# Output projection of a hybrid decoder layer: a hand-given order, squares written to SBUF, operand sums on TensorE

## The chip, the cores and the metric

One core of one Trainium2 chip. The metric is the device time of one launch in microseconds (us). Engines are named as in the profile: PE (TensorE, matmul and transpose), PEld (its weight loads), DVE (VectorE), ACT (ScalarE), POOL (GpSimd) and SP (SyncE, which here issues every transfer). Each engine works through its own queue strictly in order, and waits at an instruction whose inputs are not there.

## The reference, cut to what matters

The kernel computes one decoder layer on 1024 tokens of width 1024: a token mixer, a gated feed-forward, and a gated embedding. The change lies between the first two.

```python
mix = concatenate([ret_out, mla_out], -1) @ w_o          # 1024 x 1024
h   = x + rmsnorm(mix, post_mix_norm)
hn  = rmsnorm(h, pre_ffn_norm)
ff  = (silu(hn @ w_gate) * (hn @ w_up)) @ w_down          # inner width 2816
```

## The kernel before

Nearly every product is made three times over, from a high and a low part of each operand (`split`, L79: ACT rounds to the high part, DVE or POOL subtracts to get the low part; `products`, L89: three matmuls for each block of 128 rows).

**The output projection** runs in eight tiles of 128 tokens, in the order 0, 2, 4, 6, 1, 3, 5, 7; tile n below is the n-th of them. Half of the product (`od`) was made earlier and lies in HBM. For each tile `project` (L705) does this in turn:

- ACT and POOL split the attention rows of the tile (`mh`, `ml`), and PE makes 24 matmuls of 512 columns into a pair of PSUM banks (`po3`, two such pairs in turn).
- DVE adds the half from HBM (L715, into `mix`).
- ACT squares `mix` and sums along the row (L717). Its unwanted full-size result goes into the PSUM pair `pt`. DVE and POOL make the reciprocal root (L111, L113).
- DVE scales (L719) and adds `x` (L720, into `ht`); SP stores `ht` as the residual (`hd`).
- ACT squares `ht` (L723, again into `pt`), the root is made, DVE multiplies by the second norm's weights (L725), ACT scales (L726). `mix` now holds the tile of `hn`.

**The gate/up products** use a seven-product scheme on 2 x 2 blocks (Strassen's, Winograd's form), so `hn` is needed as seven operands: B11, B21, T2, T1, T3, B22, T4. Tiles 0 to 3 give the upper block: `operands` (L728) transposes their two halves into B11 and B21 (4 transposes of 128 x 128 each, then an ACT cast and a DVE subtraction, L681 to L688). Tiles 4 to 7 give the other five operands. T1 to T4 are differences, which POOL makes in four subtractions of 128 x 512 (L739 to L742), each before the transposes that read it.

**The gate and up weights** come in pieces of four blocks. `load` brings a piece, `weight_sums` (L791) makes three sums and a difference on POOL, `weight_part` (L798) splits a part on ACT (`gh`) and DVE (`gl`), `product(m, n)` (L820) makes product n of weight matrix m with 12 matmuls, and `evict` takes it out of PSUM. The list `steps` begins with products (0,0), (0,1), (1,0), (1,1), which need B11 and B21 alone. Step (0,2) is the first that needs T2 of all four late tiles and the sums of the weights.

**What sets the order.** A scheduler places the instructions of the output projection and of the first four products, and may mix tiles on each engine as it sees fit. From step 4 on the code stands in `tc.manual_schedule()`, where queues follow the order of the code. SP serves every load and store in one queue. Tile 7's `od` goes into the buffer that tile 4's sums read last (`blk[0]`).

Of the kernel before, what the change touches and what calls it, by code (L numbers as in the profile page):

```python
# [62 lines left out]
def hybrid_layer(ctx: ExitStack, tc: tile.TileContext, a: dict, out: bass.AP):  # L63
    nc = tc.nc
    act, dve, pool, pe, sp = nc.scalar, nc.vector, nc.gpsimd, nc.tensor, nc.sync

    const = ctx.enter_context(tc.tile_pool(name="const", bufs=1))
# [5 lines left out]
    def ps2(name):  # L73
        return ps.tile([P, 2 * 512], F32, tag="s", name=name)
# [117 lines left out]
    xt = load_in(0)  # L192
# [364 lines left out]
    def advance(gen, tag, n):  # L557
        for _ in range(n):
            try:
                gen.send(tag)  # L560
            except StopIteration:
                return
# [118 lines left out]
    def to_operand(i, j, src, tags="tfto"):  # L681
        nonlocal nblk
        pt = ps1("ptx", tags[nblk % len(tags)])
        nblk += 1
        for k in range(4):
            pe.transpose(pt[:, k * P : (k + 1) * P], src[:, k * P : (k + 1) * P], ident)
        js = slice(j * P, (j + 1) * P)
        split(xs[i][0][:, :, js], xs[i][1][:, :, js], pt.rearrange("p (k n) -> p k n", k=4))  # L688

# [7 lines left out]
    def load_rows(n):  # L697
        sp.dma_start(out=mts[n], in_=mo[order[n]])

    def load_tiles(n):  # L700
        t = order[n]
        sp.dma_start(out=blk[n % 7], in_=od[t])
        sp.dma_start(out=blk[7 + n % 3], in_=a["x"][t * P : (t + 1) * P])

    def project(n):  # L705
        t = order[n]
        mt = mts[n]
        mh, ml = [pmo.tile([P, 4, P], F32R, name=n_) for n_ in ("mh", "ml")]
        mix, ht = blk[n % 7], blk[7 + n % 3]
        split(mh, ml, mt, sub=pool)  # L710
        pt = ps2("po3")
        for c in range(2):
            cs = slice(c * 512, (c + 1) * 512)
            products(pt[:, cs], [(mh[:, k, :], ml[:, k, :], wo2[k][0][:, cs], wo2[k][1][:, cs]) for k in range(4)])
        dve.tensor_tensor(out=mix, in0=pt, in1=mix, op=ALU.add)  # L715
        ss = small.tile([P, 1], F32, name="s3")
        act.activation(pt, mix, AF.Square, accum_out=ss)  # L717
        rsqrt(ss, ss, 1.0 / D)
        dve.scalar_tensor_tensor(out=mix, in0=mix, scalar=ss, in1=wpm, op0=ALU.mult, op1=ALU.mult)  # L719
        dve.tensor_tensor(out=ht, in0=ht, in1=mix, op=ALU.add)  # L720
        sp.dma_start(out=hd[t], in_=ht)
        ss = small.tile([P, 1], F32, name="s3")
        act.activation(pt, ht, AF.Square, accum_out=ss)  # L723
        rsqrt(ss, ss, 1.0 / D)
        dve.tensor_tensor(out=mix, in0=ht, in1=wpf, op=ALU.mult)  # L725
        act.activation(mix, mix, AF.Copy, scale=ss)  # L726

    def operands(n, part=None):  # L728
        j = n % 4
        mix = blk[n % 7]  # L730
        if n < 4:
            to_operand(B11, j, mix[:, lo_])
            to_operand(B21, j, mix[:, hi_])
        else:
            e, ht = blk[j], blk[7 + n % 3]
            t1, t2, t3, t4 = e[:, lo_], ht[:, lo_], mix[:, lo_], e[:, hi_]
            b11, b12, b21, b22 = e[:, lo_], mix[:, lo_], e[:, hi_], mix[:, hi_]
            if part != 1:
                pool.tensor_tensor(out=t1, in0=b12, in1=b11, op=ALU.subtract)  # L739
                pool.tensor_tensor(out=t2, in0=b22, in1=t1, op=ALU.subtract)  # L740
                pool.tensor_tensor(out=t3, in0=b22, in1=b12, op=ALU.subtract)
                pool.tensor_tensor(out=t4, in0=b21, in1=t2, op=ALU.subtract)  # L742
            for i, src in ((T2, t2), (T1, t1), (T3, t3), (B22, b22), (T4, t4))[slice(*((0, 5), (2, 5), (0, 2))[part or 0])]:
                to_operand(i, j, src)

    load_rows(0)
    load_rows(1)
    load_tiles(0)
    for v, name in ((wpm, "w_post"), (wpf, "w_pref")):
        sp.dma_start(out=v, in_=a[name].broadcast_to([P, D]))  # L750
    for n in range(1, 4):
        if n > 1:
            load_rows(n)
        if n < 3:
            load_tiles(n)
    for n in range(NT):
        if n == 7:
            load_tiles(7)
        project(n)
        if n % 4 < 2:  # L760
            load_rows(n + (4 if n < 4 else 2))
        if n >= 2:
            operands(n - 2)
        if n < 4:
            load_tiles(n + 3)
    st_m.close()
    st_b.close()

# [29 lines left out]
    def weight_part(m, p):  # L798
        nonlocal nparts
        r, s = graw[m % 2], gs[m % 2]  # L800
        src = (r[:, 0:2], s[:, 0:2], r[:, 2:4], s[:, 2:3])[p]
        hi, lo = [v[:, : src.shape[1]] for v in ghl[nparts % 4]]
        nparts += 1
        split(hi, lo, src)
        parts[m, p] = hi, lo
# [84 lines left out]
    load(1)  # L890
    weight_part(0, 0)
    weight_part(1, 0)
    operands(NT - 2)
    for m, n in steps[:2]:
        product(m, n)
    operands(NT - 1, 2)
    for m, n in steps[2:4]:
        product(m, n)
    for m in range(2):
        weight_sums(m)  # L900
    for m, n in steps[:4]:
        evict(m, n)
# [45 lines left out]
    with tc.manual_schedule():  # L948
        for i, (m, n) in enumerate(steps):
            if i < 4:  # L950
                continue
            for f, args in todo[i]:
                f(*args)
            if i == 6:
                operands(NT - 1, 1)
            product(m, n)
            evict(m, n)
    st_g.close()
# [209 lines left out]
```

## Time and profile before

| | |
|---|---|
| median of 3 runs | 1400.54 us (1399.19 to 1403.55) |
| the profiled execution | 1400.68 us, span 1398.9 us |
| mean granted PE clock over the span | 0.986 |
| busy share of the span | PE 96%, PEld 81%, DVE 55%, ACT 39%, POOL 33% |
| output projection's first and last matmul start | 571.91 and about 635 us |
| first gate/up matmul, and step (0,2) | 644.73 and 671.25 us |
| PE without a gap again from | 671.25 us |

The profile is one execution seen from the chip. A row of a timeline has the start (us from the start of the span), the length, engine, line, operation, what is written and read, how many such instructions in a row; in brackets how long the engine had been idle before it, and what ended that. PE rows overlap, because matmuls are pipelined. A 128 x 128 float32 matmul stands as two records, a transpose as one.

### The profile page before, as it was taken

The page shows a single profiled execution, that of the slowest core. Times are in us where ns is not written, and L with a number is a line of the kernel's source. Part 1 is how long each engine was busy: PE and PEld are TensorE (multiplying, and loading weights), DVE is VectorE, ACT ScalarE, POOL GpSimd, SP SyncE. Part 2 cuts the span into 40 slices and gives each one's busy share as a digit, 9 for nine tenths or more (in the row PEclk, how much of TensorE's full clock was granted, in tenths as well). Part 3 has the DMA queues.
Part 4 walks back from the last instruction along what each step waited for, and adds up shares of the span by engine and source line. Part 5 has one row for each costly group of instructions (what it writes and reads, how often), then busy time and mean ns, then how long its engine had stood idle before and what let it go on. Part 6 is the DMA issues. An engine that isn't in the chain of part 4 may idle for free.

```text
span 1398.9 us, 18091 instructions
## 1 busy us (share of the span) xinstructions
PE 1336.5 (96%) x6756; PEld 1134.4 (81%) x6756; DVE 770.9 (55%) x1193; ACT 541.8 (39%) x898; POOL 461.8 (33%) x341
## 2 busy tenths in 40 slices
PE   7999999999989999887999999999999999999997
PEld 6987988988778887665788888888888788888886
DVE  6445637445566676488445444444445554474645
ACT  5443321011565555355343333333334444344521
POOL 1100000000363333248577666666664100012500
PEclk9999999999999999998999999999999999999999
DMA  7127831212474641743344344433346876565422
GB/s 251 46 92 250 265 118 39 75 23 60 143 232 123 200 131 30 273 135 123 121 165 149 146 173 173 169 138 144 140 178 218 269 234 211 178 218 193 138 102 75
DMA packets 85304, 214.73 MB, mean 153 GB/s; under 512 B 8992, under 2 KB 23840, under 8 KB 79584
## 3 DMA queue, kind: packets, MB, share of 16 engines
q1 hardware_dynamic: 85216, 213.58, 45.5%
q8 instruction: 53, 0.87, 0.3%
q14 instruction: 35, 0.29, 0.1%
HBM read 144.86 MB, written 67.63 MB: 152 GB/s over the span
## 4 chain that ended last, share of the span: by engine, by line
PE 83%; DMA 4%; DVE 4%; POOL 3%; issue 3%; ACT 2%; SPq 1%; DVEq 0%; ACTq 0%; POOLq 0%
PE gu L834 29%; PE db L1011 7%; PE pqk L94 6%; PE pg L94 6%; PE da L1011 6%; PE pa L94 4%; PE fill L94 3%; PE prv L94 3%; PE sc L94 3%; PE ptp L630 2%; PE prg L94 2%; PE pge L94 2%; PE po L642 1%; PE pq L94 1%; PE po L641 1%
## 5 line engine op out<-in xcount | busy, mean ns | idle before, releaser
L834 PE MATMUL gu<-x,gh 128*128 128x512 f32 x1232 | 383.6, 393 | 6.3 <-ACT po L723 5.6
L834 PEld LDWEIGHTS gu<-x,gh 128*128 128x128 f32 x1232 | 233.2, 190 | 55.7 <-ACT po L723 5.8
L834 PE MATMUL gu<-x,gl 128*128 128x512 f32 x616 | 241.2, 392 | 0.4 <-DVE gl L82 0.4
L834 PEld LDWEIGHTS gu<-x,gl 128*128 128x128 f32 x616 | 116.7, 189 | 25.1 <-DVE gl L82 0.7
L845 ACT COPY duo<-gu 128x512 f32<-128x512 f32 x66 | 38.9, 589 | 189.3 <-PE gu L834 189.3
L621 POOL TENSOR_TENSOR pr<-pr,ri 128x128 f32<-128x128 f32 (+3 forms) x64 | 74.8, 1178 | 105.7 <-DVE ri L620 98.4
L113 POOL TENSOR_TENSOR s<-s,mhalf 128x1 f32<-128x1 f32 x32 | 23.9, 752 | 238.4 <-DVE s L111 238.3
L113 POOL TENSOR_TENSOR gf<-gf,mhalf 128x4 f32<-128x4 f32 x8 | 8.1, 1008 | 266.7 <-DVE gf L111 266.7
L82 DVE TENSOR_TENSOR gl<-strip,gh 128x1024 fp32r<-128x1024 f32 (+1 forms) x44 | 61.6, 1399 | 33.3 <-ACT gh L81 33.3
L82 DVE TENSOR_TENSOR x<-draw,x 128x1024 fp32r<-128x1024 f32 (+1 forms) x43 | 48.1, 1135 | 46.9 <-ACT x L81 46.9
L82 DVE TENSOR_TENSOR gl<-graw,gh 128x1024 fp32r<-128x1024 f32 x22 | 33.8, 1538 | 72.5 <-ACT gh L81 72.5
L81 ACT CAST x<-draw 128x1024 fp32r<-128x1024 f32 (+1 forms) x47 | 45.2, 979 | 73.0 <-PE db L1011 20.6
L82 DVE TENSOR_TENSOR gl<-duo,gh 128x1024 fp32r<-128x1024 f32 x22 | 29.5, 1343 | 67.9 <-ACT gh L81 67.9
L850 DVE TENSOR_TENSOR duo<-gu,duo 128x512 f32<-128x512 f32 x66 | 45.4, 687 | 38.0 <-PE gu L834 37.9
L82 DVE TENSOR_TENSOR tl<-ptp,th 128x512 fp32r<-128x512 f32 (+1 forms) x80 | 49.8, 633 | 24.7 <-ACT th L81 23.7
L94 PE MATMUL pg<-x,x 128*128 128x512 f32 (+1 forms) x255 | 58.9, 378 | 0.0
L81 ACT CAST th<-ptp 128x512 fp32r<-128x512 f32 (+1 forms) x80 | 42.4, 544 | 41.9 <-PE ptp L630 41.6
L855 POOL TENSOR_TENSOR duo<-duo 128x512 f32<-128x512 f32 x11 | 23.3, 2122 | 103.2 <-DVE duo L818 103.2
L617 ACT ACTIVATE pr<-sc,nm 128x128 f32<-128x128 f32 (+3 forms) x64 | 47.7, 747 | 18.7 <-DVE nm L612 11.1
L94 PEld LDWEIGHTS pg<-x,x 128*128 128x128 f32 x255 | 45.8, 188 | 8.6
L612 DVE CUSTOM_DVE_ANT_0 sc<-sc,cmask 128x128 f32<-128x128 f32 (+3 forms) x64 | 48.0, 770 | 7.7 <-PE sc L94 7.3
L94 PE MATMUL pqk<-bl,hi_r 128*128 128x512 f32 x128 | 50.7, 396 | 0.0
(368 smaller groups left out, 3418.5 us busy)
## 6 DMA issues: line engine op xcount, KB each, us to landing
draw<-ld SPq DMA_DIRECT2D x58, 256.0 KB, 3.8
graw<-in_w_gate SPq DMA_DIRECT2D x11, 1024.0 KB, 8.6
duo<-in_w_up SPq DMA_DIRECT2D x11, 1024.0 KB, 4.7
duo<-in_w_down SPq DMA_DIRECT2D x11, 1024.0 KB, 5.1
td<-duo SPq DMA_DIRECT2D x11, 1024.0 KB, 4.4
ld<-duo SPq DMA_DIRECT2D x11, 1024.0 KB, 4.4
draw<-td SPq DMA_DIRECT2D x36, 256.0 KB, 4.1
ld<-duo SPq DMA_DIRECT2D x11, 768.0 KB, 6.7
```

Source lines behind the costliest of these rows:

```text
L81: act.copy(out=hi, in_=src)
L82: sub.tensor_tensor(out=lo, in0=src, in1=hi.bitcast(F32), op=ALU.subtract)
L94: pe.matmul(dst, l, r, start=(m == 0), stop=(m == n - 1))
L113: pool.tensor_tensor(out=dst, in0=dst, in1=mhalf[:, :n], op=ALU.pow)
L612: dve.tensor_tensor_reduce(out=sv, in0=sv, in1=cmask[:, S - n :].rearrange("p (c n) -> p c n", c=nc_), scale=-1.0, scalar=3.0e38, op0=ALU. ...
L617: act.activation(pr_[:, :n].rearrange("p (c n) -> p c n", c=nc_), sv, AF.Exp, bias=nm, scale=-1.0, accum_out=rs)
L621: pool.tensor_tensor(out=pr_[:, :n], in0=pr_[:, :n], in1=ri.broadcast_to([P, n]), op=ALU.mult)
L630: pe.transpose(pt[:, m * P : (m + 1) * P], pb[qq][:, kk * P : (kk + 1) * P], ident)
L834: pe.matmul(dst, l[:, at, ks], r[:, k, :], start=(n in (0, 1, 3) and x == 0), stop=(x == 11), skip_group_check=True)
L845: act.copy(out=s[nm], in_=dst)
L850: dve.tensor_tensor(out=s[nm], in0=dst, in1=s[nm], op=ALU.add)
L1011: pe.matmul(banks[j], l[:, ls], r[:, rs_], start=(fresh and q == 0 and m == 0), stop=(q == NQ - 1 and m == 2), skip_group_check=True)
```

## The change

It does five things.

1. `project` and `operands` are cut into `prepare`, `out_product`, `squares`, `sums`, `operand_list` and `turn`, and all of it, up to the first four gate/up products, stands in `tc.manual_schedule()`. In `turn(n)` three tiles are at work: tile n's norms, tile n-1's last scaling and sums, and tile n-2's operands. The matmuls of tile n+1 are queued behind tile n-2's transposes.
2. Both squares write their unwanted result to SBUF (`junk`, 8 x 128 columns in the T4 operand) and no longer to the PSUM pair.
3. POOL makes two sums a tile and not four (T1 and T3). T2 and T4 are summed by PE: a float32 matmul with the identity, or with its negative `minus`, for each of their 2 or 3 terms, added up in PSUM. For tiles 4 to 7 this makes 8 and 12 matmuls (16 and 24 records) of what were 4 and 4 transposes.
4. `minus` is made once by DVE near the program's start.
5. `load(1)`, tile 7's `od` and the weight parts stand at given places.

```diff
-        act.activation(pt, mix, AF.Square, accum_out=ss)
...
+            for n, v in enumerate(src):
+                pe.matmul(pt[:, ks], v[:, ks], (ident, minus)[n % 2], start=(n == 0), stop=(n == len(src) - 1))
...
+    def squares(n, i, v):
+        ss = roots[n, i] = small.tile([P, 1], F32, name="s3")
+        act.activation(junk, v.rearrange("p (b n) -> p b n", b=8), AF.Square, accum_out=ss)
+
+    def sums(n):
+        e, mix, ht = blk[n % 4], blk[n % 7], blk[7 + n % 3]
+        pool.tensor_tensor(out=ht[:, lo_], in0=mix[:, lo_], in1=e[:, lo_], op=ALU.subtract)
+        pool.tensor_tensor(out=ht[:, hi_], in0=mix[:, hi_], in1=mix[:, lo_], op=ALU.subtract)
...
+        return [(T2, j, (b22, t1)), (T1, j, (t1,)), (T3, j, (t3,)), (B22, j, (b22,)), (T4, j, (b21, b22, t1))]
...
+    def turn(n):
+        mix, ht = blk[n % 7], blk[7 + n % 3]
+        own, last = n < NT, 1 <= n
+        ops = operand_list(n - 2) if n >= 2 else []
+        if own:
+            dve.tensor_tensor(out=mix, in0=banks_o[n], in1=mix, op=ALU.add)
+        if last:
+            rsqrt(roots[n - 1, 1], roots[n - 1, 1], 1.0 / D)
+        for o in ops[:2]:
+            to_operand(*o)
+        if own:
+            squares(n, 0, mix)
+        if last:
+            act.activation(blk[(n - 1) % 7], blk[(n - 1) % 7], AF.Copy, scale=roots[n - 1, 1])
+        if own:
+            rsqrt(roots[n, 0], roots[n, 0], 1.0 / D)
+        if n - 1 >= 4:
+            sums(n - 1)
+        for o in ops[2:]:
+            to_operand(*o)
+        if own:
+            if n + 2 < NT:
+                prepare(n + 2)
+            if n + 1 < NT:
+                out_product(n + 1)
+            dve.scalar_tensor_tensor(out=mix, in0=mix, scalar=roots[n, 0], in1=wpm, op0=ALU.mult, op1=ALU.mult)
+            dve.tensor_tensor(out=ht, in0=ht, in1=mix, op=ALU.add)
+            sp.dma_start(out=hd[order[n]], in_=ht)
+            squares(n, 1, ht)
+            dve.tensor_tensor(out=mix, in0=ht, in1=wpf, op=ALU.mult)
...
+        for n in range(NT - 1):
+            turn(n)
+            if n < 4:
+                load_tiles(n + 3)
+            if n in (2, 3):
+                load_rows(n + 4)
+            if n == 6:
+                load_tiles(7)
...
+    with tc.manual_schedule():
+        turn(NT - 1)
+        load(1)
+        weight_part(0, 0)
+        for m, n in steps[:2]:
+            product(m, n)
+        turn(NT)
+        weight_part(1, 0)
+        for m, n in steps[2:4]:
+            product(m, n)
+        for o in operand_list(NT - 1)[:2]:
+            to_operand(*o)
+        for m in range(2):
+            weight_sums(m)
```

Three places show what moves. SP's queue at the last tiles, before (`hd` is a store of the residual, `duo<-od` and `duo<-in_x` are loads of a tile, `graw<-in_w_gate` is the first gate weights' load):

```order
L703 DMA duo_5742<-in_x 128x1024
L721 DMA hd_91<-duo_5742 128x1024
L789 DMA graw<-in_w_gate 128x2048
L702 DMA duo_5741<-od_109 128x1024
L789 DMA duo_5738<-in_w_up 128x2048
L721 DMA hd_93<-duo_5742 128x1024
```

and in the change:

```order
L773 DMA hd_88<-duo_5744 128x1024
L773 DMA hd_90<-duo_5741 128x1024
L773 DMA hd_92<-duo_5744 128x1024
L710 DMA duo_5743<-od_110 128x1024
L711 DMA duo_5744<-in_x 128x1024
L823 DMA graw<-in_w_gate 128x2048
L773 DMA hd_94<-duo_5744 128x1024
L823 DMA duo_5740<-in_w_up 128x2048
```

Tile 7's `od` stands behind tile 6's store in both. Its `x` moved behind that store, the gate weights behind both loads, and the up weights behind tile 7's store.

ACT's queue from the last tile's norms to the first parts of the weights, before (`x_5730` to `x_5734` are T2, T1, T3, B22, T4; `gh` casts are parts of the weights; L717 and L723 are tile 7's squares):

```order
L81 CAST gh_6262<-graw 128x1024
L81 CAST x_5733<-ptx 128x4x128
L81 CAST x_5731<-ptx 128x4x128
L717 ACTIVATE po_6173,s_6199<-duo_5741 128x1024
L81 CAST x_5730<-ptx 128x4x128
L81 CAST gh_6256<-duo_5738 128x1024
L81 CAST x_5732<-ptx 128x4x128
L845 COPY duo_5739<-gu 128x512
L723 ACTIVATE po_6173,s_6206<-duo_5742 128x1024
```

and in the change (`x_5732` to `x_5736` are now T2, T1, T3, B22, T4; L729 is tile 7's second square, L759 its last scaling):

```order
L729 ACTIVATE x_5736,s_6289<-duo_5744 128x8x128
L81 CAST gh_6223<-graw 128x1024
L81 CAST x_5732<-ptx 128x4x128
L81 CAST x_5733<-ptx 128x4x128
L759 ACTIVATE duo_5743<-duo_5743,s_6289 128x1024
L81 CAST x_5734<-ptx 128x4x128
L81 CAST x_5735<-ptx 128x4x128
L81 CAST x_5736<-ptx 128x4x128
L81 CAST gh_6217<-duo_5740 128x1024
L81 CAST gh_6219<-strip 128x1024
L81 CAST gh_6221<-strip 128x1024
L81 CAST x_5732<-ptx 128x4x128
```

The cast of the first gate part moved from before tile 7's squares to behind both of them. Tile 7's own T2 cast (the last row) stands behind the casts of the summed parts `gh_6219` and `gh_6221` of both weight matrices.

POOL's queue at the same place, before (L739 to L742 are tile 7's sums, L793 to L796 the sums of weights, L113 the roots):

```order
L793 TENSOR_TENSOR strip<-graw 128x512
L794 TENSOR_TENSOR strip<-strip,graw 128x512
L796 TENSOR_TENSOR graw<-graw 128x512
L795 TENSOR_TENSOR strip<-graw,strip 128x512
L794 TENSOR_TENSOR strip<-strip,duo_5738 128x512
L113 TENSOR_TENSOR s_6206<-s_6206,mhalf 128x1
L795 TENSOR_TENSOR strip<-duo_5738,strip 128x512
L739 TENSOR_TENSOR duo_5741<-duo_5741 128x512
```

and in the change (L733 and L734 are tile 7's sums, L827 to L830 the sums of weights):

```order
L113 TENSOR_TENSOR s_6289<-s_6289,mhalf 128x1
L733 TENSOR_TENSOR duo_5744<-duo_5743 128x512
L734 TENSOR_TENSOR duo_5744<-duo_5743 128x512
L827 TENSOR_TENSOR strip<-graw 128x512
L828 TENSOR_TENSOR strip<-strip,graw 128x512
L829 TENSOR_TENSOR strip<-graw,strip 128x512
L830 TENSOR_TENSOR graw<-graw 128x512
L827 TENSOR_TENSOR strip<-duo_5740 128x512
L828 TENSOR_TENSOR strip<-strip,duo_5740 128x512
```

The sums of weights moved from before tile 7's last root and sums to behind them.

## Rows read from the trace of the kernel before

**Rows 1.** Who waited for whom, 575 to 700 us: total us, times, longest.
```profile
PE po L94 <- ACT po L723: 9.2, 6, 3.6
...
PE gu L834 <- ACT po L723: 5.6, 1, 5.6
```

**Rows 2.** Stretches: us, busy time by engine, then granted PE clock, DMA share, GB/s.
```profile
600.00:610.00 10.00, 7.56 (x22) 6.00 (x23) 7.24 (x9) 3.82 (x6) 1.16 (x3) 0.66 0.55 182
...
670.00:680.00 10.00, 9.32 (x33) 6.93 (x32) 2.30 (x2) 2.53 (x4) 4.97 (x5) 0.68 0.30 105
680.00:690.00 10.00, 10.00 (x49) 8.40 (x48) 6.41 (x8) 4.97 (x10) 8.21 (x6) 1.00 0.86 285
```

**Rows 3.** Chain that ended last, from step 4 of the gate/up products on.
```profile
680.87 59.20 PE gu L834 x261
```

**Rows 4.** Timeline of DVE in the output projection.
```profile
578.06 1.22 DVE L715 TENSOR_TENSOR duo<-po,duo 128x1024 f32<-128x1024 f32 x1 [5.26 <-PE po L94]
...
597.65 1.28 DVE L719 SCALAR_TENSOR_TENSOR duo<-duo,s,strip 128x1024 f32<-128x1024 f32 x1 [0.66 <-POOL s L113]
598.97 2.17 DVE L720 TENSOR_TENSOR duo<-duo,duo 128x1024 f32<-128x1024 f32 x1
601.06 1.21 DVE L715 TENSOR_TENSOR duo<-po,duo 128x1024 f32<-128x1024 f32 x1
...
606.71 1.23 DVE L720 TENSOR_TENSOR duo<-duo,duo 128x1024 f32<-128x1024 f32 x1
...
613.70 1.27 DVE L82 TENSOR_TENSOR x<-ptx,x 128x512 fp32r<-128x512 f32 x2
...
627.52 1.21 DVE L715 TENSOR_TENSOR duo<-po,duo 128x1024 f32<-128x1024 f32 x1
...
646.33 1.21 DVE L715 TENSOR_TENSOR duo<-po,duo 128x1024 f32<-128x1024 f32 x1
```

**Rows 5.** Timeline of ACT: a square and its sum, a scaling, a cast of weights.
```profile
595.64 1.05 ACT L717 ACTIVATE po<-duo 128x1024 f32<-128x1024 f32 x1
596.60 0.20 ACT L717 ACTIVATION_READ_ACCUMULATOR po<-duo 128x1 f32 x1
...
614.44 1.15 ACT L726 ACTIVATE duo<-duo,s 128x1024 f32<-128x1024 f32 x1 [0.15 <-POOL s L113]
...
677.31 1.05 ACT L81 CAST gh<-graw 128x1024 fp32r<-128x1024 f32 x1
```

**Rows 6.** Timeline of POOL: a low part of the rows, and a sum of weights.
```profile
598.58 1.48 POOL L82 TENSOR_TENSOR ml<-strip,mh 128x512 fp32r<-128x512 f32 x1 [0.96 <-ACT mh L81]
...
660.26 1.28 POOL L795 TENSOR_TENSOR strip<-graw,strip 128x512 f32<-128x512 f32 x1
```

**Rows 7.** Timeline of PE: float32 matmuls (two records each), projection, transposes, gate/up.
```profile
333.21 1.05 PE L475 MATMUL pu<-vt,kz 128*128 128x128 f32 x8
...
585.16 0.50 PE L94 MATMUL po<-bh,mh 128*128 128x512 f32 x1 [2.21 <-ACT po L723]
...
602.44 0.79 PE L94 MATMUL po<-bh,mh 128*128 128x512 f32 x1 [3.58 <-ACT po L723]
603.03 0.63 PE L94 MATMUL po<-bl,mh 128*128 128x512 f32 x1
...
644.73 0.71 PE L834 MATMUL gu<-x,gh 128*128 128x512 f32 x2
...
671.25 1.52 PE L834 MATMUL gu<-x,gh 128*128 128x512 f32 x2 [0.68 <-ACT x L81]
...
679.39 1.47 PE L686 MATMUL ptx<-pack,duo 128*128 128x128 f32 x12
680.62 0.71 PE L834 MATMUL gu<-x,gh 128*128 128x512 f32 x2
```

**Rows 8.** DMA issues with KB and us to landing: tile 7's `od`, and an `x` alone.
```profile
duo<-od SPq DMA_DIRECT2D x1, 512.0 KB, 7.3
...
duo<-in_x SPq DMA_DIRECT2D x1, 512.0 KB, 3.6
```

More of the change, by code (lines that the diff above doesn't have):

```diff
@@ L123, in hybrid_layer @@
     mhalf = const.tile([P, 32], F32, name="mhalf")
+    minus = const.tile([P, P], F32, name="minus")
     pool.memset(mhalf, -0.5)
@@ L654, in hybrid_layer @@
     act.activation(small.tile([P, 1], F32, name="warm", bufs=1), rs, AF.Silu)
+    dve.tensor_scalar(out=minus, in0=ident, scalar1=-1.0, scalar2=None, op0=ALU.mult)
     advance(gen, "f", 2 * NT)
@@ L685, in to_operand @@
         for k in range(4):
-            pe.transpose(pt[:, k * P : (k + 1) * P], src[:, k * P : (k + 1) * P], ident)
+            ks = slice(k * P, (k + 1) * P)
+            if len(src) == 1:
+                pe.transpose(pt[:, ks], src[0][:, ks], ident)
+                continue
+            for n, v in enumerate(src):
+                pe.matmul(pt[:, ks], v[:, ks], (ident, minus)[n % 2], start=(n == 0), stop=(n == len(src) - 1))
         js = slice(j * P, (j + 1) * P)
@@ L703, in load_tiles, with prepare, out_product @@
         sp.dma_start(out=blk[7 + n % 3], in_=a["x"][t * P : (t + 1) * P])
[L705 to L711, printed above, removed]
+    junk = xt[6][:, :, :, 3 * P :].rearrange("p h k n -> p (h k) n")
+    split_rows, banks_o, roots = {}, {}, {}
+    def prepare(n):
+        split_rows[n] = [pmo.tile([P, 4, P], F32R, name=n_) for n_ in ("mh", "ml")]
+        split(*split_rows[n], mts[n], sub=pool)
+    def out_product(n):
+        mh, ml = split_rows[n]
+        pt = banks_o[n] = ps2("po3")
         for c in range(2):
@@ L714, in project, with operand_list @@
             products(pt[:, cs], [(mh[:, k, :], ml[:, k, :], wo2[k][0][:, cs], wo2[k][1][:, cs]) for k in range(4)])
-        dve.tensor_tensor(out=mix, in0=pt, in1=mix, op=ALU.add)
-        ss = small.tile([P, 1], F32, name="s3")
-        act.activation(pt, mix, AF.Square, accum_out=ss)
[L718 to L728, printed above, removed]
+    def squares(n, i, v):
[5 more added lines that the diff above has]
+        pool.tensor_tensor(out=ht[:, hi_], in0=mix[:, hi_], in1=mix[:, lo_], op=ALU.subtract)
+    def operand_list(n):
         j = n % 4
@@ L731, in operands @@
         if n < 4:
[L732 to L744, printed above, removed]
+            return [(B11, j, [mix[:, lo_]]), (B21, j, [mix[:, hi_]])]
+        e, ht = blk[j], blk[7 + n % 3]
+        b21, b22, t1, t3 = e[:, hi_], mix[:, hi_], ht[:, lo_], ht[:, hi_]
+        return [(T2, j, (b22, t1)), (T1, j, (t1,)), (T3, j, (t3,)), (B22, j, (b22,)), (T4, j, (b21, b22, t1))]
[29 more added lines that the diff above has]
+            dve.tensor_tensor(out=mix, in0=ht, in1=wpf, op=ALU.mult)
     load_rows(0)
@@ L750, in hybrid_layer @@
         sp.dma_start(out=v, in_=a[name].broadcast_to([P, D]))
[L751 to L765, printed above, removed]
+    load_rows(2)
+    load_tiles(1)
+    load_rows(3)
+    load_tiles(2)
+    with tc.manual_schedule():
+        prepare(0)
+        load_rows(4)
+        prepare(1)
+        load_rows(5)
+        out_product(0)
+        for n in range(NT - 1):
[6 more added lines that the diff above has]
+                load_tiles(7)
     st_m.close()
@@ L889, in hybrid_layer @@
     load(0)
[L890 to L902, printed above, removed]
+    with tc.manual_schedule():
+        turn(NT - 1)
[11 more added lines that the diff above has]
+            weight_sums(m)
+        for m, n in steps[:4]:
+            evict(m, n)
     for q in range(NQ):
@@ L951, in hybrid_layer @@
                 continue
+            if i == 6:
+                for o in operand_list(NT - 1)[2:]:
+                    to_operand(*o)
             for f, args in todo[i]:
                 f(*args)
-            if i == 6:
-                operands(NT - 1, 1)
             product(m, n)
```

## The prediction

> **What bounds the kernel now.** I read the chain that ended last first. From step 4 of the gate/up products on it is PE alone: 261 matmuls in 59.20 us, 0.227 each, without a gap [rows 3]. The stretches say the same: PE is busy 10.00 of 10 us in 680 to 690, but 7.56 of 10 in 600 to 610 [rows 2]. So whatever brings step (0,2) forward or back moves the rest of the kernel by as much, and only the stretch from 572 to 680 us counts. Next I read who waits for whom there: PE waits 9.2 us for ACT's second square (L723) to release the projection's PSUM pair, and 5.6 us more for the same line before the first products of the up weights [rows 1]. These waits are what the change can take. The timelines of the engines then give the price of every piece. In the projection, DVE starts a new tile (L715) at 578.06 for tile 0 and at 627.52 for tile 6, 8.2 us a tile, and tile 7 follows only at 646.33 [rows 4]. Yet PE has only 24 matmuls and 8 transposes to do for an early tile: 24 x 0.227 + 8 x 0.10 = 6.2 us (12 transposes take 1.23 from 679.39 to the product's start at 680.62 [rows 7]).
>
> **The change, part by part.** I follow the new queues to the start of step (0,2).
>
> *Tiles 0 to 6.* With the squares in SBUF, PE no longer waits for ACT. But what is late next is the norm's own chain, which no order shortens. From L715's start: the square begins after 1.24, takes 1.21 with its sum [rows 5], and 0.85 later (596.80 to 597.65) L719 starts [rows 4, 5]. L719 to L720 is 1.32, L720 takes 2.09 (598.97 to 601.06), L725 some 1.14. This is 7.85 us. Beside the first two steps DVE's two operand subtractions, 1.27 [rows 4], fit. I take 2.09 for L720 because in the new order POOL's low part `ml` for tile n+2 waits for ACT's cast behind the last scaling, and so falls on L719 and L720 in each turn, as the `ml` of 598.58 fell on the L720 of 598.97. Undisturbed, L720 took 1.23 at 606.71 [rows 4, 6]. The square's new form, float32 to strided SBUF, is in no row. Its nearest rows are the square to PSUM, 1.05, and the scaling to SBUF, 1.15 [rows 5]: I add 0.1. Six turns of 7.95 are 47.7, and turn 5 pays 1.3 more for POOL's first sums beside DVE: tile 6's L715 starts at 578.1 + 47.7 + 1.3 = 627.1, against 627.52. **Nothing is gained here.**
>
> *Tile 7's load.* SP's queue holds tile 7's `od` behind tile 6's store, and that behind tile 6's L720. In the new DVE queue L719 and L720 of tile 6 stand behind all five operands of tile 4. PE's part of these is 16 + 4 + 4 + 4 + 24 = 52 records. Eight float32 records took 1.05 [rows 7], about 0.11 each with the last one's tail left out: 5.8 us. They begin when T1's sum is there, at about 623.7, and end at 629.5, or at 631.9 if the clock has fallen by then. With cast and subtraction, L719 runs at about 633, L720 ends at 635.6, and the load is issued at 636. Alone 512 KB landed in 3.6, beside a load of weights in 7.3 [rows 8]. Here a store and `x` run with it, which is nearer to the first: I take 5. Tile 7's L715 starts at 641.2, **5.1 earlier** than 646.33 [rows 4].
>
> *The first gate product.* Here the order loses. Before, it started at 644.73 [rows 7], ahead of tile 7's L715. Now its weight cast stands on ACT behind both of tile 7's squares, and these behind tile 5's operands: after L715 one subtraction gives T4 its PSUM bank (1.8), T4's 24 records take 2.7, its cast and subtraction 1.4, L719 1.5, L720 1.2, the square 1.2, the cast 1.05 [rows 4, 5, 7]. That is 11 us: start at **652.2**, 7.5 later.
>
> *To the last scaling.* Two products are 24 matmuls, 5.4. PE has then been idle for some 6 us. In the rows, after an idle of 3.58 us the matmuls of 602.44 and 603.03 stand at 0.79 and 0.63, where that of 585.16, after 2.21, stands at 0.50, and the granted clock of 600 to 610 is 0.66: 2.4 GHz for a part of it and 1.2 for the rest [rows 2, 7]. At 1.2 GHz a matmul takes 0.227 more. I add 2.4, about eleven such matmuls. T2 of tile 6, 16 records, follows at 660.0 and ends at 661.8. Its cast and T1's are 1.1, and then ACT comes to tile 7's scaling, 1.15 [rows 5], at **664.1**.
>
> *POOL's tail.* Behind that scaling POOL has two sums for tile 7 and then the weight sums of both matrices, of which six must be done before the second matrix's part can be cast. Eight times 1.33 (one takes 1.28 [rows 6]) is 10.7. Two meet a DVE subtraction of weights, 1.1 each, as `ml` and L720 met [rows 4, 6]. This ends at 677.0. The cast takes 1.05 [rows 5], and T2 of tile 7 stands behind it on ACT, and behind that part's subtraction on DVE: 0.5 + 1.1 + 0.7 more. Step (0,2) starts at **680.4**, 9.1 after 671.25 [rows 7].
>
> *Behind it.* T3, B22 and T4 of tile 7 are now 32 records, 3.6 us, where 12 transposes took 1.23 [rows 7]: 2.4 more on PE. The low clock after 671.25 (0.68 in 670 to 680 [rows 2]) was paid before and is paid again, since PE idles ahead of (0,2) as it did.
>
> The sum: 9.1 + 2.4 = **11.5 us**, against the profiled execution's 1400.68: 1412.2, and the median shown is 0.14 lower. I say **1412**.
>
> *At nothing:* `minus`, one 128-wide DVE instruction while the program's first loads are awaited, under 0.3 us were it bare. POOL's eight sums fewer: POOL waits for the scaling, not for itself, until the tail. The extra records of tiles 4 and 5 lie under the wait for tile 7's `od`. If that cover went, they would cost 40 x 0.11 = 4.4 us, of which 4 are in the sum already, through L719 of tile 6.
>
> *Bounds.* Float32 matmuls that ran one by one, at about 0.2 a record, would add some 4 us on the path. At half my price they'd take off 2.5. The square's form: 0 to 1. The load of `od`: 3.6 to 7.3, so -1.4 to +2.3. The clock: two falls of 2.4, neither or both. The meetings of POOL and DVE: from none (-9, below) to one more in each late turn (+4).
>
> **Rivals.** *Faster: POOL and DVE do not meet, and the clock stays up.* Then L720 is 1.23 in seven turns (-6), the sums and the weight sums meet nothing (-3.5), the first products run at 2.4 GHz, before (0,2) too (-4.8), and the load comes early (-1.4): 1412 - 15.7 = **1396**. For it: before, L720 met `ml` only in some turns, and 606.71 shows the clean one. Against it: in the new order `ml` is released just there in every turn. It decides for this case if five or more of the eight L720 are under 1.3. The Trainium skill (SBUF — State Buffer, section "SBUF: two separate sides") says that DVE and GpSimd lock their shared SBUF ports for a whole instruction, so whoever starts first blocks the other. By this an `ml` that came after L720's start would only hand the same delay to L725, and the turn would stay as long; the trace agrees, with 2.17 against 1.23.
>
> *About even: half the meetings vanish and one fall of the clock,* 1412 - 8 = **1404**.
>
> *Slower still: PE's clock falls in the projection itself.* PE idles about 1.7 us in each turn of 7.95. If that were enough to hold the clock down, 24 matmuls at 0.45 are 10.9 us with 8 transposes 1 to 2 more, and PE would set a turn of 12: six turns give 6 x 4 = 24, of which the wait for tile 7's load hides 4: **1432**. For it: the row of 602.44. Against: after the 2.21 of 585.16, more than a turn's single gaps, the matmul stood at 0.50 [rows 7].
>
> *The change doesn't do what it says:* the queues show that it does, but for the weight casts ahead of tile 7's T2, which is in the sum.
>
> **How the numbers follow.** A measurement of this kernel tells about 0.3% (4.2 us) from no change. The forecast, 1406 to 1420, has 0.70, all of it slower. The even case has 0.13, half within 0.3% and half slower. The fast rival has 0.11, of which 0.09 is faster and 0.02 the same. The slow one has 0.06. Sums: faster 0.09, same 0.09, slower 0.82. The range that leaves out the fast rival and most of the slow one is 1400 to 1423.
>
> **What would show it.** Right: L715 of tile 6 near 627 and of tile 7 near 641; L720 near 2.1 in most turns; the first gate product at 652, PE idle for 5 us and more ahead of it; tile 7's scaling at 664; POOL at work without a gap from there for 12 us; step (0,2) near 680. Wrong: a turn of 7 us or less, or step (0,2) before 672, which would make the change even or faster. PE's wait for ACT's square should be gone in any case.

## The result, and the profile after

| | before | the change |
|---|---|---|
| median of the runs of the first comparison | 1400.27 us (5 runs) | 1413.74 us (5 runs, 1406.31 to 1416.29) |
| ratio, with 95% interval | | 1.0091, 1.0067 to 1.0115 |
| the profiled execution, its span | 1400.68, 1398.9 | 1406.31, 1404.5 |
| PE busy, granted PE clock over the span | 96%, 0.986 | 96%, 0.991 |
| DVE, ACT, POOL busy | 55%, 39%, 33% | 55%, 39%, 32% |

The change is slower by 0.7 to 1.2%. Its profiled execution happens to be the quickest of the five; a second series with a second profile stands below (`change_again`: 1.0069, 1.0046 to 1.0093). As tile 0's first add (L715, now L751) starts at another time in each execution, the text counts from there. Three stretches then make the span: up to that add (578.06 before, 574.92 in the change), from it to ACT's copy of product (0,3) (108.33 and 116.78), and the rest (712.5 and 712.8). **The change shows in the middle one.** The first wanders by more than its 3.1 between executions (last section).

Who waited for whom from 572 to 690 us in the change (us in total, times, longest), where [rows 1] had PE waiting for ACT's squares:

```profile
POOL duo L733 <- ACT duo L759: 10.5, 4, 9.8
...
PE gu L868 <- ACT gh L81: 7.6, 2, 6.0
...
DVE duo L751 <- DMA duo<-od: 3.6, 1, 3.6
...
PE gu L868 <- DVE duo L884: 2.4, 1, 2.4
```

PE's waits for the squares are gone. In their place PE waits 6.0 for the first gate part's cast, POOL 9.8 for tile 7's scaling, and DVE 3.6 for tile 7's `od`. The chain of waits of the change joins these (start, length, engine, what is written, line; pieces under 0.4 us are left out, other cuts are marked):

```profile
631.53 1.23 DVE duo L772
633.21 4.34 DMA duo<-od
637.63 1.22 DVE duo L751
...
645.09 1.24 DVE duo L772
646.41 1.15 ACT x L729 x2
647.56 0.94 ACT gh L81
648.52 1.22 DVE gl L82
649.82 6.48 PE gu L868 x22
656.30 1.80 PE ptx L694 x16
658.12 1.07 ACT x L81 x2
659.20 1.05 ACT duo L759
660.32 1.27 POOL duo L733
...
671.31 1.29 POOL strip L828
672.62 1.05 ACT gh L81
673.70 1.33 DVE gl L82
675.03 1.20 DVE x L82 x2
676.23 0.61 DVE duo L884
676.88 5.75 PE gu L868 x24
682.63 0.87 PE ptx L690 x8
683.50 2.68 PE ptx L694 x24
686.18 73.94 PE gu L868 x326
```

It is one serial chain through five engines: tile 6's residual, tile 7's load, its norms, the gate cast, both first products, tile 6's T2, tile 7's scaling, eight POOL operations in a row, a cast, two subtractions, an eviction (L884), and only then step (0,2) at 676.88. From 686.18 on PE is alone, as in [rows 3].

DVE, ACT, PE and POOL of the change, timelines that answer to [rows 4, 5, 7, 6]:

```profile
590.92 1.22 DVE L751 TENSOR_TENSOR duo<-po,duo 128x1024 f32<-128x1024 f32 x1
...
594.30 1.28 DVE L771 SCALAR_TENSOR_TENSOR duo<-duo,s,strip 128x1024 f32<-128x1024 f32 x1 [0.73 <-POOL s L113]
595.62 2.18 DVE L772 TENSOR_TENSOR duo<-duo,duo 128x1024 f32<-128x1024 f32 x1
...
598.98 1.22 DVE L751 TENSOR_TENSOR duo<-po,duo 128x1024 f32<-128x1024 f32 x1
```

```profile
646.41 1.06 ACT L729 ACTIVATE x<-duo 128x1024 fp32r<-128x1024 f32 x1 [3.27 <-DVE duo L772]
...
674.07 1.07 ACT L81 CAST x<-ptx 128x512 fp32r<-128x512 f32 x2 [0.39 <-PE ptx L694]
```

```profile
648.54 1.22 PE L868 MATMUL gu<-x,gh 128*128 128x512 f32 x2 [6.03 <-ACT gh L81]
...
676.88 0.73 PE L868 MATMUL gu<-x,gh 128*128 128x512 f32 x2 [2.42 <-DVE duo L884]
```

```profile
595.07 1.65 POOL L82 TENSOR_TENSOR ml<-strip,mh 128x512 fp32r<-128x512 f32 x1 [0.80 <-ACT mh L81]
...
664.12 2.28 POOL L828 TENSOR_TENSOR strip<-strip,graw 128x512 f32<-128x512 f32 x1
```

The square to SBUF takes 1.06, to PSUM it took 1.05 [rows 5]. L772 of 595.62 met POOL's low part of 595.07 and took 2.18, and a turn is 8.06 (590.92 to 598.98). Two stretches (busy us of PE, PEld, DVE, ACT and POOL, then the granted clock) answer to [rows 2]: 640 to 650 is the gap before the first product, and in 670 to 680, where before had 0.68, the clock is now 1.00.

```profile
640.00:650.00 10.00, 3.94 (x26) 3.02 (x25) 7.18 (x10) 4.77 (x9) 3.09 (x4) 0.78 0.37 133
...
670.00:680.00 10.00, 7.58 (x44) 6.41 (x43) 4.51 (x6) 3.78 (x7) 6.00 (x4) 1.00 0.00 0
```

### The profile page after: what moved, and what is told of

The parts are those of the page before. It is cut to its first block, busy times and chain, and to the rows that moved or that the text cites. A ratio compares the mean times of both kernels' runs of the same rounds, so it can differ in the third digit from the quotient of the medians.

```text
span 1404.5 us, 18353 instructions
## 1 busy us (share of the span) xinstructions
PE 1344.7 (96%) x6884; PEld 1143.5 (81%) x6884; DVE 770.0 (55%) x1194; ACT 541.1 (39%) x898; POOL 445.4 (32%) x333
## 4 chain that ended last, share of the span: by engine, by line
PE 83%; DVE 5%; issue 4%; ACT 3%; POOL 2%; DMA 2%; SPq 1%; DVEq 0%; ACTq 0%; POOLq 0%
PE gu L868 29%; PE db L1049 8%; PE pqk L94 6%; PE pg L94 6%; PE da L1049 6%; PE pa L94 4%; PE fill L94 3%; PE prv L94 3%; PE sc L94 3%; PE ptp L631 2%; PE prg L94 2%; PE pge L94 2%; PE pq L94 1%; PE po L643 1%; DVE duo L772 1%
## 5 line engine op out<-in xcount | busy, mean ns | idle before, releaser
L113 POOL TENSOR_TENSOR s<-s,mhalf 128x1 f32<-128x1 f32 x32 | 23.9, 750 | 265.8 <-DVE s L111 265.8
L113 POOL TENSOR_TENSOR gf<-gf,mhalf 128x4 f32<-128x4 f32 x8 | 8.1, 1006 | 266.7 <-DVE gf L111 266.7
L884 DVE TENSOR_TENSOR duo<-gu,duo 128x512 f32<-128x512 f32 x66 | 45.4, 688 | 38.8 <-PE gu L868 37.5
```

Source lines behind the costliest of these rows:

```text
L884: dve.tensor_tensor(out=s[nm], in0=dst, in1=s[nm], op=ALU.add)
```

## The experiments

Theory: the order around tile 7 and the first products costs the time. Rivals: the extra float32 records on PE, the squares' new place, and POOL's tail or PE's clock alone. "Kernel before" means the runs of it on the same chip in the same series. The kernel before had a median of 1400.27 in the first series, 1398.14 beside `change_again` to `weight_sums_first`, 1396.07 beside `low_part_dve` to `sums_alone`, 1398.25 beside `scheduled` and `two_norms`, and 1395.76 beside the last two: compare ratios, not medians, across series. The last four columns are starts in us after tile 0's first add, from one profile each ("scaling" is tile 7's last):

| kernel | median | ratio to before (95%) | tile 7's add | scaling | step (0,2) | copy of (0,3) |
|---|---|---|---|---|---|---|
| before | 1400.27 | 1 | 68.27 | 86.70 | 93.19 | 108.33 |
| the change | 1413.74 | 1.0091 (1.0067 to 1.0115) | 62.71 | 84.17 | 101.96 | 116.78 |
| change_again | 1408.85 | 1.0069 (1.0046 to 1.0093) | 62.78 | 87.09 | 104.87 | 121.32 |
| gate_first | 1407.15 | 1.0059 (1.0039 to 1.0078) | 63.32 | 80.72 | 98.50 | 114.91 |
| pool_sums | 1408.33 | 1.0060 (1.0037 to 1.0083) | 66.84 | 88.18 | 103.10 | 117.31 |
| weight_sums_first | 1410.08 | 1.0077 (1.0058 to 1.0095) | 62.80 | 84.21 | 101.71 | 116.52 |
| low_part_dve | 1408.28 | 1.0094 (1.0066 to 1.0121) | 62.03 | 84.63 | 102.41 | 118.83 |
| load_first | 1407.18 | 1.0092 (1.0064 to 1.0119) | 59.56 | 83.46 | 101.25 | 117.70 |
| squares_alone | 1397.91 | 1.0018 (1.0000 to 1.0037) | 65.02 | 86.06 | 92.65 | 107.94 |
| sums_alone | 1396.01 | 1.0008 (0.9989 to 1.0027) | 62.96 | 77.29 | 87.52 | 103.33 |
| scheduled | 1396.37 | 0.9986 (0.9970 to 1.0003) | 63.15 | 83.02 | 90.56 | 105.96 |
| two_norms | 1390.58 | 0.9937 (0.9913 to 0.9962) | 56.39 | 69.16 | 87.88 | 100.93 |
| tail_only | 1401.72 | 1.0040 (1.0024 to 1.0056) | 64.29 | 76.01 | 95.10 | 111.49 |
| head_only | 1407.20 | 1.0076 (1.0056 to 1.0096) | 56.43 | 80.06 | 97.84 | 114.27 |

The first seven below "before" are the change, or the change with one edit. `squares_alone`, `sums_alone` and `scheduled` are the kernel before with parts of the change. The last three have a mended hand order.

**change_again**: the change, unedited.

> The change once more, for its spread. From tile 0's first add (L751) to the start of step (0,2) the change took 101.96 us in its profile, the kernel before 93.19. If the order costs the time, this stretch is again 102 within 1 us and the median again near 1413. If the loss is only in where PE's clock falls, the stretch changes by more than 3 us between two profiles of the same kernel.

Neither came true as written. The order's stretch is long again, but 104.87 is not within 1 us of 102, nor is the median near 1413; and the two profiles of one kernel differ by 2.9 in it, not by more than 3, though by 4.5 up to the copy of (0,3). PE in this profile:

```profile
640.77 0.78 PE L694 MATMUL ptx<-pack,duo 128*128 128x128 f32 x2 [2.13 <-DVE x L82]
...
651.37 1.22 PE L868 MATMUL gu<-x,gh 128*128 128x512 f32 x2 [6.03 <-ACT gh L81]
...
680.92 0.73 PE L868 MATMUL gu<-x,gh 128*128 128x512 f32 x2 [4.03 <-DVE duo L884]
...
682.94 1.05 PE L868 MATMUL gu<-x,gh 128*128 128x512 f32 x2
```

The waits are the change's own (6.03 again, and L884), but the clock fell elsewhere. A pair of matmuls stands at 0.62 at 2.4 GHz; here (0,2) has pairs at 1.05 (1.2 GHz) after an idle of 4.03, where the first profile had full speed after 2.42. The length of the wait alone does not tell: after 2.16 at the same place the 24 matmuls of (0,2) ran at full speed in `weight_sums_first` (5.58 us) and fell to 1.2 GHz for a part in `tail_only` (7.32). A median of this kernel is taken over executions that can differ so.

**gate_first**: the first gate part ahead of tile 7's second square.

```diff
+            if n == NT - 1:
+                weight_part(0, 0)
             dve.scalar_tensor_tensor(out=mix, in0=mix, scalar=roots[n, 0], in1=wpm, op0=ALU.mult, op1=ALU.mult)
...
         load(1)
-        weight_part(0, 0)
```

> The first gate part's cast moves ahead of tile 7's second square, its subtraction ahead of tile 7's L771, at a price of 1.2 us for tile 7's own norms. Theory 'order': the first gate product starts near 69.5 us after tile 0's first add where the change had 73.6, step (0,2) near 97 where it had 102.0, and the median falls by about 5, to 1409. Rival 'float32 records on PE cost it': no gain above 1 us, 1413 or, with the 1.2 us, 1415.

The first product started at 69.82 (73.62 and 75.32 in the two profiles of the change), step (0,2) 3.5 to 6.4 earlier. The median is 1.7 under `change_again`, and the two intervals overlap: the profile moved as expected, the time can't tell.

**pool_sums**: T2 and T4 summed by POOL again, in the hand order.

```diff
-        pool.tensor_tensor(out=ht[:, lo_], in0=mix[:, lo_], in1=e[:, lo_], op=ALU.subtract)
-        pool.tensor_tensor(out=ht[:, hi_], in0=mix[:, hi_], in1=mix[:, lo_], op=ALU.subtract)
+        pool.tensor_tensor(out=e[:, lo_], in0=mix[:, lo_], in1=e[:, lo_], op=ALU.subtract)
+        pool.tensor_tensor(out=ht[:, lo_], in0=mix[:, hi_], in1=e[:, lo_], op=ALU.subtract)
+        pool.tensor_tensor(out=mix[:, lo_], in0=mix[:, hi_], in1=mix[:, lo_], op=ALU.subtract)
+        pool.tensor_tensor(out=e[:, hi_], in0=e[:, hi_], in1=ht[:, lo_], op=ALU.subtract)
```

> All four operand sums back on POOL, the hand order kept. Rival 'float32 records on PE cost it': most of the 13 us comes back, 1402 or less. Theory 'order': 20 records fewer behind step (0,2) give 2.2 us, two more sums in POOL's tail for tile 7 take 2.6, so 1412 to 1416.

1408.33 beside 1408.85 of the change in the same series (the expectation's figures stood on the first series' 1413): nothing came back, so the float32 records are not most of the loss. As POOL pays for it here, this run can't price the records by themselves; `sums_alone` and `scheduled` do. In this run POOL's four sums of tile 4 take 7.8 us (621.81 to 629.63) and hold tile 6's root behind them, and tile 7's load is issued at 60.96 instead of 58.29.

**weight_sums_first**: four of POOL's eight operations taken out of the tail.

```diff
+        if n == NT:
+            weight_sums(0)
         if n - 1 >= 4:
             sums(n - 1)
```

> The first matrix's four weight sums move ahead of tile 7's two sums on POOL, where POOL waited 9.8 us for tile 7's scaling. Theory 'POOL's tail sets step (0,2)', which is the step in the prediction: step (0,2) is 5 us or more earlier, median 1408. Rival 'PE's own queue sets it' (the first products, tile 6's operands and the up products, one behind the other): tile 7's T2 cast waited only 0.39 us for PE behind the weight cast, so POOL's 6 us less give 0.4 us or nothing, median 1413.

The rival was right on the step. ACT of this kernel, at the cast of tile 7's T2, and POOL at tile 7's sums:

```profile
675.93 1.07 ACT L81 CAST x<-ptx 128x512 fp32r<-128x512 f32 x2 [6.53 <-PE ptx L694]
```

```profile
662.23 1.28 POOL L733 TENSOR_TENSOR duo<-duo 128x512 f32<-128x512 f32 x1 [3.57 <-ACT duo L759]
```

The cast waits 6.53 for PE, where the change had 0.39: POOL is done 6 us sooner and PE's queue is as late as ever. From tile 7's scaling to (0,2) it is 17.50 instead of 17.79. POOL's tail and PE's queue were **two chains of nearly one length**, and shortening one gave 0.3. That holds where the up products ran partly at 1.2 GHz, as here and in the first profile (8.0 us for their 24 matmuls). In `change_again` they took 6.4, PE's transposes for T2 ended at 676.46, and the cast at 677.62 was 1.2 behind them: there POOL's tail was the longer one.

**low_part_dve**: DVE makes `ml` in its gap behind the operand subtractions.

```diff
+        if n + 2 < NT:
+            high_part(n + 2)
         if own:
             dve.tensor_tensor(out=mix, in0=banks_o[n], in1=mix, op=ALU.add)
...
         if own:
             squares(n, 0, mix)
+        if n + 2 < NT:
+            low_part(n + 2)
...
-                prepare(n + 2)
```

> DVE makes the low part ml in its own gap behind the operand subtractions, and POOL no longer meets L772. Theory 'the meeting sets the turn': L772 is 1.23 us in all turns, a turn 7.1 to 7.3 us where it was 8.0, tile 6's first add 4 to 5 us earlier, and the median 4 us lower, 1409. Rival 'the delay only moves to L775 or to PE': turns of 7.8 or more, 1413.

Missed. L772 (L782 in this kernel) took 1.23 in every turn but turn 5, and turns 2 to 4 took 7.6 for 8.06, but tile 6's add came only 0.6 earlier (48.60 for 49.17). DVE's own `ml`, 0.68, takes back about half of the 0.95 that L782 saves in those turns. ACT and DVE show where the rest went:

```profile
577.01 0.62 ACT L722 CAST mh<-duo 128x512 fp32r<-128x512 f32 x1 [9.16 <-DMA duo<-mo]
```

```profile
616.95 2.28 DVE L781 SCALAR_TENSOR_TENSOR duo<-duo,s,strip 128x1024 f32<-128x1024 f32 x1 [0.73 <-POOL s L113]
619.26 2.17 DVE L782 TENSOR_TENSOR duo<-duo 128x1024 f32<-128x1024 f32 x1
```

The early cast waited for its load and held tile 0's first square behind it (a first turn of 9.25), and in turn 5 both norm steps, L781 and L782, now meet POOL's operand sums (9.52 for 9.01).

**load_first**: tile 7's loads ahead of tile 6's store.

```diff
+        if n == 6:
+            load_tiles(7)
         if own:
...
-            if n == 6:
-                load_tiles(7)
```

> Tile 7's two loads are issued ahead of tile 6's residual store, as soon as T4 of tile 4 has read the buffer. Theory 'order': the load is issued some 3.5 us earlier, tile 7's first add starts 3.5 us earlier (62.7 us after tile 0's in the change, now 59), step (0,2) too, median 1410. Rival 'the add would wait for something else': less than 1 us.

Tile 7's add came 3.2 earlier, as expected; it now waits for the projection itself:

```profile
634.95 1.22 DVE L751 TENSOR_TENSOR duo<-po,duo 128x1024 f32<-128x1024 f32 x1 [0.43 <-PE po L94]
```

Step (0,2) is 0.7 earlier than in the change's first profile and 3.6 than in the second, whose first products ran as slowly as here (12.9 us from the first product to the end of tile 7's scaling, 11.7 in the first profile). The ratio shows nothing of it.

**squares_alone** and **sums_alone**: the kernel before with one edit each, the scheduler free.

```diff
-        act.activation(pt, mix, AF.Square, accum_out=ss)
+        act.activation(junk, mix.rearrange("p (b n) -> p b n", b=8), AF.Square, accum_out=ss)
```

```diff
-                pool.tensor_tensor(out=t2, in0=b22, in1=t1, op=ALU.subtract)
-                pool.tensor_tensor(out=t4, in0=b21, in1=t2, op=ALU.subtract)
-            for i, src in ((T2, t2), (T1, t1), (T3, t3), (B22, b22), (T4, t4))[slice(*((0, 5), (2, 5), (0, 2))[part or 0])]:
+            for i, src in ((T2, (b22, t1)), (T1, (t1,)), (T3, (t3,)), (B22, (b22,)), (T4, (b21, b22, t1)))[slice(*((0, 5), (2, 5), (0, 2))[part or 0])]:
```

> The kernel before with the squares written to SBUF and nothing else; the scheduler orders the rest. Theory 'order': the squares' place is no loss, PE's 5.6 us of wait ahead of the up products goes, and part of it arrives at step (0,2): 1396 to 1400. Rival 'the strided write to SBUF costs time': a square of 1.3 us or more and 1402 or more.

> The kernel before with T2 and T4 summed on PE and nothing else. Theory 'order': 20 more records behind step (0,2) cost 2.2 us, one POOL sum less ahead of tile 7's T2 gives 1.3 back: 1400 to 1403. Rival 'float32 records on PE cost it': 1408 or more.

`squares_alone` fell into its range, `sums_alone` 4 under its own; the kernel before, too, was 4 lower in that series (1396.07). Against before the loss of either is at most 0.4% (1.0037, 1.0027), and none is shown. With the squares in SBUF alone tile 6's add comes at 36.9 instead of 49.5, but tile 7's at 65.0 (68.3 before): its load is issued at 61.0, no earlier than before (58.5), as its buffer is read by tile 4's transposes until then. Then PE waits at tile 7's operands:

```profile
666.25 1.11 PE L686 MATMUL ptx<-pack,duo 128*128 128x128 f32 x4 [7.63 <-POOL duo L741]
```

With the sums on PE alone the stage is 5.0 shorter in the profile than that of before, yet the medians are equal. One profile each can't settle that.

**scheduled**: both edits, without the hand order (the two diffs together).

> The kernel before with both edits, squares in SBUF and T2 and T4 summed on PE, but the scheduler's order and not the hand's. Theory 'the hand order costs it': no slower than the kernel before, 1393 to 1399 beside 1396 to 1398, and from tile 0's first add to the eviction of step (0,3) 103 to 108 us (before 108.3, the change 116.8 and 121.3). Rival 'the two edits cost it together': 1405 or more.

Theory confirmed: 0.9986, and the copy of (0,3) at 105.96. The edits of points 2 to 4 of the change cost nothing that the interval allows to see (1.0003 at most); **the hand order, points 1 and 5, costs it all.**

**two_norms**: the hand order mended in all these places at once. Tile 7's `od` goes into the strip's last third (`third`), free since turn 5. Not shown in the cut: DVE makes `ml`, POOL makes tile 7's T4 again, and the weight sums and the evictions of (0,0) and (1,0) stand ahead of tile 7's T2.

```diff
+        sp.dma_start(out=third, in_=od[order[7]])
...
+        to_operand(*t2)
+        first_square(6)
+        scaling(5)
+        root(6, 0)
+        late = to_operand(*t4, later=True)
+        sums(5)
+        out_product(7)
+        sp.dma_start(out=blk[0], in_=a["x"][order[7] * P : (order[7] + 1) * P])
+        norm1(6)
+        residual(6)
+        second_square(6)
+        late()
+        norm2(6)
...
+        turn7()
+        load(1)
+        root(7, 1)
+        scaling(7)
+        sums(7)
+        last = operand_list(6)
+        for o in last[:2]:
+            to_operand(*o)
+        weight_part(0, 0)
+        for o in last[2:]:
+            to_operand(*o)
+        for m, n in steps[:2]:
+            product(m, n)
```

> The hand order mended where the experiments point: tile 7's half from HBM is loaded into the strip's last third, free since turn 5, its x behind T4 of tile 4 alone; L772 of tile 6 no longer stands behind tile 4's operands, tile 7's scaling stands ahead of tile 6's, the first products behind those; DVE makes ml, POOL T4 of tile 7, the first evictions stand ahead of tile 7's T2. Theory 'these places cost the time': tile 7's first add near 56 us after tile 0's (62.7 in the change), step (0,2) near 84 (102.0; before 93.2), the eviction of step (0,3) near 97 (116.8; before 108.3), and the median 8 to 11 us under the kernel before, 1386 to 1390. Rival 'PE's clock or DVE takes the gain': step (0,2) at 92 or later, the median at that of before or above.

It beats both kernels: 0.9937, some 9 us under before by the ratio, 7.7 by the medians of that series (1390.58 and 1398.25; 8 to 11 were expected). Tile 7's add is at 56.39 as expected, (0,2) at 87.88 and the copy of (0,3) at 100.93, both 4 later than expected: PE waits four times, 1.05 to 1.55, for DVE's operand subtractions. As it changes who makes `ml` and T4 too, its gain over `scheduled` is not the order's alone. Around step (0,2) PE now waits 0.24 and 0.23:

```profile
664.86 0.49 PE L951 MATMUL gu<-x,gh 128*128 128x512 f32 x1 [0.24 <-ACT x L697]
665.59 0.50 PE L951 MATMUL gu<-x,gh 128*128 128x512 f32 x1 [0.23 <-DVE x L698]
```

**tail_only** and **head_only**: two halves of that. `tail_only` is the change with the new order behind tile 7's turn; `head_only` has the turns and loads of `two_norms` and the change's order behind them. POOL's T4 for tile 7 and the evictions ahead of its T2 are in neither.

```diff
         turn(NT - 1)
         load(1)
-        weight_part(0, 0)
-        for m, n in steps[:2]:
-            product(m, n)
-        turn(NT)
+        mix = blk[(NT - 1) % 7]
+        rsqrt(roots[NT - 1, 1], roots[NT - 1, 1], 1.0 / D)
+        ops = operand_list(NT - 2)
+        for o in ops[:2]:
+            to_operand(*o)
+        weight_part(0, 0)
+        act.activation(mix, mix, AF.Copy, scale=roots[NT - 1, 1])
+        sums(NT - 1)
+        for o in ops[2:]:
+            to_operand(*o)
+        for m, n in steps[:2]:
+            product(m, n)
```

> The change up to tile 7's turn, word for word, and behind it the other order: tile 6's operands and tile 7's scaling ahead of the first products, the first gate part's cast between tile 6's second and third operand. Theory 'the order behind tile 7's turn costs the time': tile 7's first add unchanged at 62.7, its scaling near 75 us after tile 0's first add (84.2 to 87.1 in the change), step (0,2) near 91 (102 to 105), the eviction of step (0,3) near 105 (116.8 to 121.3), the median 8 to 12 us under the change and within 0.3% of the kernel before. Rival 'the projection's turns and tile 7's load cost it': 3 us or less under the change.

> The other half: turns 0 to 7 as in the mended order, tile 7's loads too, and behind them the change's own order (first gate part and products, then tile 6's operands, tile 7's scaling, sums, weight sums, the up products). Theory 'the turns and tile 7's load cost the time': first add of tile 7 at 56.4, step (0,2) near 86 to 90, median near that of the fully mended order, 1391 to 1394. Rival 'the order behind tile 7's turn costs it': the 6 us of the add arrive and no more, step (0,2) near 95 to 98, the median 4 to 8 us under the change.

The tail is the larger half: 1.0040 against 1.0069 and 1.0091, scaling at 76.01, (0,2) at 95.10 (expected 91; PE waited 3.13 for DVE's subtractions). It is less than the 8 to 12 us expected and does not reach the kernel before. Its tile 7's add is 1.6 later than the change's, though the code up to there is the same: T4 of tile 4 took PE 4.6 us, 2.7 in the change. The head brings tile 7's add to 56.43 and (0,2) to 97.84, but no time that can be told from the change's. Each acts in its own stretch: from tile 7's add to step (0,2) it is 30.8 us with the tail, 41.4 with the head and 31.5 in `two_norms` (39.3 and 42.1 in the change). At step (0,2) the halves save 7 to 10 and 4 to 7 us, both together 14 to 17: about the sum.

In time they don't add up: 0.3 to 0.5% for the tail, 0.2% at most for the head, 1.3 to 1.5% for both. `two_norms` alone of the three keeps PE at full clock from 650 to 690 (1.00, the halves 0.91), has 20 records less in T4 of tile 7, and has the first evictions out of the way. In the halves (0,2) still waits for them, first `tail_only`, then `head_only`:

```profile
671.91 0.90 PE L868 MATMUL gu<-x,gh 128*128 128x512 f32 x2 [2.16 <-DVE duo L884]
```

```profile
677.36 0.73 PE L947 MATMUL gu<-x,gh 128*128 128x512 f32 x2 [4.04 <-DVE duo L963]
```

Which of these three gives the rest, no run shows.

## Why the prediction was right

The prediction's times, less its 578.06 for tile 0's add, beside the two profiles of the change:

| step of the prediction | predicted | the change | change_again |
|---|---|---|---|
| tile 6's add | 49.0 | 49.17 | 49.17 |
| tile 7's load issued | 57.9 | 58.29 | 58.29 |
| tile 7's add | 63.1 | 62.71 | 62.78 |
| first gate product | 74.1 | 73.62 | 75.32 |
| end of tile 7's scaling | 86.0 | 85.33 | 88.25 |
| step (0,2) | 102.3 | 101.96 | 104.87 |
| copy of (0,3), as 108.33 + 11.5 | 119.8 | 116.78 | 121.32 |

- *Tiles 0 to 6, nothing gained*: right, with L720 (now L772) at 2.17 to 2.19 in five turns, 2.09 predicted, and a turn of 8.06 for 7.95. The Trainium skill (SBUF — State Buffer, section "SBUF: two separate sides") has a DVE instruction with two SBUF inputs and a GpSimd instruction lock their shared ports for a whole instruction; the trace agrees, 2.18 beside POOL and 1.23 without. `low_part_dve` shows what taking the meeting away buys: L782 is 1.23 in turns 1 to 4, but DVE's own `ml` costs half of that, and in turn 5 POOL's sums meet L781 and L782. Two small slips change nothing: the square with its sum is 1.16 in [rows 5], not 1.21, and the rival's 6 and 3.5 for the meetings make 9.5, not 9.
- *Tile 7's first add, 5.1 earlier*: right (5.6 earlier than before), by its own steps. The load itself is issued no earlier, 58.29 for 58.45 before. It lands in 4.3 (5 predicted) instead of 7.3 [rows 8], and DVE takes it up at once, where before DVE stood in a weight subtraction (644.07, 2.33 long).
- *The first gate product, 7.5 later*: right (73.62 and 75.32 against 66.67 before), behind the waits named. The 11 us from tile 7's add took 10.9 and, with T4's records of 640.77 at 1.2 GHz for a part, 12.5.
- *To the last scaling*: right. From the first product to the scaling's end 11.9 were predicted, with one fall of the clock; it took 11.7 and 12.9, and the first products began at 1.2 GHz in both (pairs at 1.05).
- *POOL's tail, 16.3 from the scaling's end to (0,2)*: 16.6 in both profiles, with the two meetings as written (L828 and L830 at 2.28 and 2.26). But this fits by two errors that cancel: POOL's eight took 12.3 up to the cast, not 12.9, and 4.3 followed from there to the step, not 3.4, since an eviction (L884, 0.61) stands on DVE between T2's subtraction and the step, which the sum left out. And PE's queue ended within 0.4 us of that tail in the first profile (1.2 in the second): that POOL sets the end was true by a hair, and gave no lever in `weight_sums_first`.
- *Behind it*: 2.4 for T4's records was right: T3, B22 and T4 took 3.46 (682.47 to 685.93), against 1.23, so 2.2. That "the low clock is paid again" was wrong in the first profile (1.00 in 670 to 680), and half right in the second.

In the first profile that clock is 2.55 of the 3.0 missing in the last row: the 24 matmuls from (0,2) to the next transposes took 5.59 at full speed, 8.14 before (7.21 in the second profile).

So the mechanism was right up to step (0,2), within 0.4 us in the first profile. That 1412 lies 1.7 us from the first median is luck in part: the stretch up to the copy of (0,3) lost 8.5 us in one profile and 13.0 in the other, for 11.5 predicted, and the medians of the two series stand 13.5 and 10.7 above the kernel before.

The rival *faster* fell as foreseen: of eight L772 three were under 1.3, not five. *Slower still* did not come: PE idled in every turn, and the clock stood at 1.00 from 570 to 620. As the prediction had it, the change gains up to tile 7's add (5.6) and loses behind it: **from that add to step (0,2)** it is 24.9 us before, 39.3 and 42.1 in the change, and 27.4 in `scheduled`. What it could not say is that the loss belongs to the order alone: it charged 2.4 of 11.5 to the records, and with them in the scheduler's order nothing is lost.

Left open: why `gate_first`, which moved step (0,2) by 3.5 to 6.4 us, showed 1.7 us in the median. The intervals are some 3 us to either side, and the two profiles of the change are 4.5 apart, so the runs can't tell a small gain from none.

## What to carry to other kernels

A hand order fixes not only what comes early but what queues behind it: follow each in-order queue through the last tile, and name for every engine the one instruction that a late input holds up. Where two chains end within a microsecond of each other, mend both before judging either. When an edit comes with a new order, time the edit in the old order too: here the edits alone were even and the order alone was the loss. A mended order, with `ml` on DVE and one sum back on POOL, was a gain.

## What the runs showed of the hardware

The start of tile 0's first add wandered from 574.01 to 580.72 us over these profiles, though their queues hardly differ ahead of it. In the earliest (`low_part_dve`), stretches of 50 us had granted clocks of 1.00, 0.97, 1.00 and 1.00 from 400 to 600; in the latest (`gate_first`) 0.93, 1.00, 1.00 and 0.90. So the same work ran behind PE's gaps at 2.4 GHz in one execution and partly at 1.2 GHz in another. The medians of the change in two series differ by 4.9 (1413.74 and 1408.85); that the clock makes all of that is not shown, as only one execution of each series has a profile.
